# The opening of a transformer layer's kernel, written as one fixed list of steps on three engines

## The chip, the cores and the metric

The kernel runs as one program on one core of a Trainium2 chip. A core has a matrix engine (TensorE, PE in the profile), a vector engine (VectorE, DVE), a scalar engine (ScalarE, ACT), GpSimd (POOL) and queues for DMA, most of them issued here from SyncE (SP). Each engine works through its own instructions in the order in which they stand in the program, and waits on semaphores for the others.

The metric is device time in microseconds (us) of one launch. Before the change three runs took 3028.93, 3019.19 and 3015.33 us: a median of 3019.19 us.

## The reference, cut to what matters

One layer of a diffusion backbone: 2048 latent tokens and 256 context tokens of width 1024. Only its start matters here:

```python
mod_x = silu(c) @ w_mod + b_mod                    # shift, scale, gate rows
sh1, sc1, g1, sh2, sc2, g2 = split(mod_x, 6)
h_x = rmsnorm(x, norm1_g) * (1 + sc1) + sh1        # modulate
p_x = h_x @ w_in                                   # 1024 x 3840: K | V | Q | u | v | two gates
k_x = rope(rmsnorm(p_x[:, :128])); v_x = p_x[:, 128:256]
q_x = rope(rmsnorm(p_x[:, 256:768]))
...                                                # attention, gMLP, gates, output, MLP
```

## The kernel before

**The tiling.** Tokens go in blocks of 512. The input projection multiplies two blocks at a time by a 2 x 2 scheme of seven products instead of eight (Strassen's, in Winograd's form): the two token blocks are the rows of the scheme, the two halves of the 1024 inner elements are its inner index, and two neighbouring groups of columns are its columns. The first column group pair is K, V and Q, 768 columns as two of 384 (`pairs[0]`, tile width n = 384). The products are taken in the order `SUMS = (0, 1, 5, 6, 4, 2, 3)`. Product 0 and product 1 need only the first token block and raw weights. The third product taken (number 5), the fourth (6) and the later ones need differences of both blocks and differences of weights, which VectorE makes.

**Split operands.** Every fp32 factor goes to TensorE as a rounded high part (a ScalarE copy with rounding) and a low part (a VectorE subtraction of the high part), and each product of tiles is three matmuls: high by high, high by low, low by high. One product is done in two chunks of two 128-row pieces of the inner index each, and a chunk has 2 x 4 token tiles x 3 = 24 matmuls of 128x384.

**What the opening has to do before the first product.** The modulation rows are made in four quarters q = 0 to 3 (two 128-channel pieces each): 8 narrow matmuls over `w_mod` (`mod_row`, L345), a ScalarE copy of the row (L349), 4 transposes (L207 from `mod_finish`), a VectorE reduction and three small VectorE steps that leave shift S1 and scale G1 (L357 to L368). Then the 1024 channels of the normalized first block are turned, 128 channels by 512 tokens at a time: 4 transposes into one PSUM bank (`turn`, L207), then a ScalarE pass that applies G1 and S1 on the way out (L558). ScalarE and VectorE split the result (`operand`, L593 and L594), and TensorE multiplies. For the second block ScalarE first squares 8 half rows (L526), VectorE makes the inverse root (13 small steps, L172 to L188, L533) and scales 8 half rows (L543), and then the block is turned in the same way. Differences of the blocks are L604 and L605 (`h_five`), weight differences L642, their split L652 and L654.

**PSUM.** Four banks (tag `a`) hold the four token tiles of the product that runs; four (tag `b`) take everything else in turn: modulation rows, transposes, filling matmuls. Filling matmuls (`fill`, L202: ones by the identity) are put in where TensorE would otherwise stand still. Between products a partial sum is copied out of the `a` banks (L745 for product 0, L750 for products 5 and 6); after product 1 each token tile is copied out (L2255), sent to HBM (L2259, issued on ScalarE's queue) and the bank is loaded again with the sum of product 0 (L748).

**What sets the order.** `project` writes the opening as a generator, `opening()`, whose pieces are taken one by one by `pairs_run` through `hook`, between the matmuls of the first products. The instructions recorded in `self.pins` keep the order in which they are written on every engine; SP's loads keep theirs (`self.loads`). `self.fences` closes the stretch: what comes after stays behind it on TensorE and VectorE. The pinned stretch ends with the operands of product 5. After it the weight differences of product 6 and 3 and their stores (L658, from where later chunks are read back at L731) and the operands of product 6 (`h_sums`) are recorded as ordinary work.

**Loads.** SP issues in the order: head, first block x0, then for each quarter a 384 KB piece of `w_in` (L715) and 8 pieces of `w_mod` of 256 KB (L332), with the second block x1 ahead of quarter 2, and last the 16 pieces of `w_in` for the weight differences (L636). Each load waits on one of eight semaphores in turn, and so for the load eight places ahead of it.

Of the kernel before, what the change touches and what calls it, by code (L numbers as in the profile page):

```python
# [2 lines left out]

# [7 lines left out]
F32R = mybir.dt.float32r  # L11
# [59 lines left out]
LAST_ON_VECTOR = (2, 4, 7, 8, 9, 12, 13, 14, 15)  # L71

# [9 lines left out]
class Kern:  # L82
# [253 lines left out]
    def mod_row(self, w, ahead=0, between=0):  # L336
# [11 lines left out]
        row = self.t2([TB])  # L348
        nc.scalar.copy(row, ps)  # L349
        return row, pt  # L350

    def mod_finish(self, row, pt, q):
        nc = self.nc
        bcol, gcol = self.mod_cols
        self.transposes(pt, [row[:, j * P : (j + 1) * P] for j in range(2 * MQ)])
# [159 lines left out]
    def h_scale(self, xs, dve=False):  # L515
        for _ in self.h_apply(xs, self.h_rstd(xs, self.h_squares(xs)), dve):
            pass

    def h_squares(self, xs):
        nc = self.nc  # L520
        nt, parts = len(xs), len(xs[0])
        ss = self.small([parts, TT])
        for t in range(nt):
            for n, x in enumerate(xs[t]):
                junk = self.t2([D], mybir.dt.bfloat16)[:, : x.shape[-1]]
                nc.scalar.activation(junk, x, AF.Square, accum_out=ss[:, n, t : t + 1])  # L526
        return ss
# [10 lines left out]
    def h_apply(self, xs, r, dve):  # L538
        nc = self.nc
        for t in range(len(xs)):  # L540
            for x in xs[t]:
                if dve:
                    nc.vector.tensor_scalar(  # L543
                        out=x, in0=x, scalar1=r[:, t : t + 1], scalar2=None, op0=ALU.mult
                    )
                else:
                    nc.scalar.activation(x, x, AF.Copy, scale=r[:, t : t + 1])
                yield

# [4 lines left out]
    def turn(self, xs, k, out, fill=0):  # L554
        ps = self.bank([TB])
        self.fill(ps, fill)
        self.transposes(ps, [self.columns(x, k) for x in xs])
        self.nc.scalar.activation(  # L558
            out, ps, AF.Identity, scale=self.G1[:, k, 0:1], bias=self.S1[:, k, 0:1]
        )  # L560
# [47 lines left out]
    def h_sums(self, raw, h, fives):  # L608
        tt = self.nc.vector.tensor_tensor
        for k0 in range(0, HK, 2):  # L610
            for kk in (k0, k0 + 1):
                if fives:
                    self.h_five(raw, h, kk)
            yield
        for p, i, j in ((6, 0, 0), (4, 1, 0), (2, 0, 1), (3, 1, 1)):
# [10 lines left out]
    def opening_terms(self, pair, direct):  # L626
        nc = self.nc
        tt, sub = nc.vector.tensor_tensor, ALU.subtract
        n, w = pair.n, self.I["w_in"][0]
        b, t = {}, {}  # L630
        for kk in range(HK):
            for k in (kk, kk + HK):
                r = [self.h2([n]) for _ in range(2)]
                for j in range(2):
                    lo = pair.lo + j * n
                    nc.sync.dma_start(r[j], w[k * P : (k + 1) * P, lo : lo + n])  # L636
                b[k] = [r[j] for j in pair.cols]
        yield

        def term(p, kk, in0, in1):  # L640
            t[p, kk] = self.sb("hx", [n])
            tt(out=t[p, kk], in0=in0, in1=in1, op=sub)  # L642

        def first(kk):
            term(4, kk, b[kk][1], b[kk][0])
            term(5, kk, b[kk + HK][1], t[4, kk])

        def split(p, c):
            hi, lo = self.f4([2, n], F32R), self.f4([2, n], F32R)
            direct.append([(hi[:, s], lo[:, s]) for s in range(2)])  # L650
            for s in range(2):
                nc.scalar.copy(hi[:, s], t[p, 2 * c + s])  # L652
            for s in range(2):
                tt(out=lo[:, s], in0=t[p, 2 * c + s], in1=f32(hi[:, s]), op=sub)  # L654

        def store(p):
            for kk in range(HK):
                nc.sync.dma_start(self.t_d[pair.index][p][kk // 2][kk % 2], t[p, kk])  # L658

        first(0)  # L660
        yield
        first(1)
        yield
        split(5, 0)
        yield
        first(2)
        first(3)
        yield
        split(5, 1)
# [1902 lines left out]
```

## Time and profile before

| | us |
|---|---|
| runs: median, lowest, highest | 3019.19, 3015.33, 3028.93 |
| the profiled execution's own time | 3016.04 |
| its span (first to last instruction) | 3013.9 |
| TensorE busy in the span | 2938.2 (97%) |
| VectorE busy | 2084.8 (69%) |
| ScalarE busy | 1420.9 (47%) |
| GpSimd busy | 662.1 (22%) |
| DMA queue q1, share of 16 engines | 53.7% |

TensorE is busy nearly all the time, so its idle time is where the time is to be looked for. The page's row of 40 slices (75 us each) shows it for TensorE: 7 tenths in the first slice, 8 in the second, 9 (90% or more) in all others.

### The profile page before, as it was taken

Reading aid. Unit: us, or ns where it says so; the run is one execution under the profiler, and the core shown is the slowest. Engines: PE = TensorE matmul, PEld = TensorE weight load, DVE = VectorE, ACT = ScalarE, POOL = GpSimd, SP = SyncE. Lnnn points to the kernel's source line nnn. Section 1 sums busy time; section 2 is a strip of 40 time slices with the busy share of each in tenths; the row PEclk is TensorE's granted clock in tenths of the full one; section 3 lists DMA queues with packets and bytes.
Section 4 is the critical chain, followed back from the end, with each engine's and each line's share of the span. In section 5 each row is a group of like instructions: output and inputs, shape, how many; then the busy total and the mean of one; then the engine's idle time right before and its main releaser. Section 6 shows DMA issues by size and latency. Waiting matters only on the chain. (4 is left out here: it accounts for less than half of the span.)

```text
span 3013.9 us, 38296 instructions
## 1 busy us (share of the span) xinstructions
PE 2938.2 (97%) x13489; PEld 2227.6 (74%) x13489; DVE 2084.8 (69%) x2998; ACT 1420.9 (47%) x2328; POOL 662.1 (22%) x470
## 2 busy tenths in 40 slices
PE   7899999999999999999999999999999999999999
PEld 6778888876555555546888878888887888888887
DVE  4867387766888898897555587776676766654555
ACT  5645765554544545554222354444454344444432
POOL 0000000000999899895111200000000000000000
PEclk9999999999999999999999999999999999999999
DMA  7587967775010010116776658888766544447554
GB/s 268 169 298 247 321 212 217 249 245 178 24 36 27 24 37 22 30 39 195 225 219 190 184 196 306 302 306 304 260 218 223 185 154 154 154 160 270 210 209 155
DMA packets 386720, 559.06 MB, mean 185 GB/s; under 512 B 38672, under 2 KB 192448, under 8 KB 386528
## 3 DMA queue, kind: packets, MB, share of 16 engines
q1 hardware_dynamic: 374224, 535.90, 53.7%
q10 hardware_dynamic: 12304, 20.71, 1.8%
q8 instruction: 106, 1.74, 0.2%
q14 instruction: 86, 0.70, 0.1%
HBM read 379.75 MB, written 176.69 MB: 185 GB/s over the span
## 5 line engine op out<-in xcount | busy, mean ns | idle before, releaser
L2387 DVE TENSOR_REDUCE ts<-b 128x1 f32<-128x512 f32 x492 | 302.0, 683 | 62.2 <-PE b L2376 62.2
L2472 POOL TENSOR_TENSOR ac<-ac,p 128x512 f32<-128x512 f32 x214 | 317.0, 1511 | 46.4 <-ACT p L2444 46.4
L1990 DVE TENSOR_TENSOR b<-b,b 128x1024 fp32r<-128x1024 f32 x170 | 200.9, 1222 | 138.2 <-ACT b L1989 137.9
L1989 ACT CAST b<-b 128x1024 fp32r<-128x1024 f32 x170 | 170.7, 1051 | 225.8 <-PE b L1874 100.1
L2444 ACT ACTIVATE p<-b 128x512 f32<-128x512 f32 x384 | 193.5, 625 | 166.6 <-PE b L2440 158.8
L1873 PE MATMUL b<-b,b 128*128 128x512 f32 x680 | 265.3, 390 | 3.8 <-DVE b L1990 3.8
L1872 PE MATMUL b<-b,b 128*128 128x512 f32 x680 | 266.2, 391 | 2.7 <-DVE f L2011 1.4
L1874 PE MATMUL b<-b,b 128*128 128x512 f32 x680 | 264.7, 389 | 0.0
L2472 POOL TENSOR_TENSOR ac<-p,p 128x512 f32<-128x512 f32 x32 | 54.9, 1736 | 748.6 <-ACT p L2444 748.5
L2472 POOL TENSOR_TENSOR ac<-ac,t 128x512 f32<-128x512 f32 x152 | 202.7, 1361 | 0.0
L2421 PE MATMUL b<-h,h 128*128 128x512 f32 x576 | 185.9, 403 | 2.1 <-ACT m L2303 0.9
L2452 PE MATMUL b<-p,h 128*64 128x512 f32 x768 | 184.8, 604 | 0.0
L2440 PE MATMUL b<-h,h 128*128 128x512 f32 x576 | 178.1, 390 | 0.0
L1873 PE MATMUL b<-hb,b 128*128 128x512 f32 x446 | 173.8, 390 | 0.0
L1882 DVE TENSOR_TENSOR f<-f,b 128x512 f32<-128x512 f32 x160 | 109.3, 683 | 79.9 <-issue 46.3
L1872 PE MATMUL b<-hb,b 128*128 128x512 f32 x415 | 161.9, 390 | 0.9 <-DVE f L1882 0.9
L1874 PE MATMUL b<-hb,b 128*128 128x512 f32 x415 | 161.3, 389 | 0.0
L1873 PEld LDWEIGHTS b<-b,b 128*128 128x128 f32 x680 | 127.7, 188 | 32.4 <-DVE b L1990 5.8
L1872 PEld LDWEIGHTS b<-b,b 128*128 128x128 f32 x680 | 127.6, 188 | 31.1 <-ACT b L1989 3.9
L2421 PEld LDWEIGHTS b<-h,h 128*128 128x128 f32 x576 | 103.4, 188 | 61.4 <-DVE ts L2387 24.3
L1874 PEld LDWEIGHTS b<-b,b 128*128 128x128 f32 x680 | 127.6, 188 | 26.4
L166 POOL TENSOR_TENSOR bw<-bw,bw 128x512 fp32r<-128x512 f32 x58 | 76.3, 1336 | 235.6 <-ACT bw L162 235.6
(451 smaller groups left out, 7278.3 us busy)
## 6 DMA issues: line engine op xcount, KB each, us to landing
ao_d<-f SPq DMA_DIRECT2D x224, 256.0 KB
f<-in_w_ff SPq DMA_DIRECT2D x48, 1024.0 KB
b<-ao_d SPq DMA_DIRECT2D x85, 512.0 KB
b<-w2o_d SPq DMA_DIRECT2D x85, 512.0 KB
w2o_d<-f SPq DMA_DIRECT2D x112, 256.0 KB
f<-in_w_in SPq DMA_DIRECT2D x38, 512.0 KB
f<-x_d SPq DMA_DIRECT2D x64, 256.0 KB
hb<-ao_d SPq DMA_DIRECT2D x54, 256.0 KB
```

The lines of the kernel that those rows point to most:

```text
L1872: mm(ps, wh, hh, start=start and k == 0, stop=False, skip_group_check=True)
L1873: mm(ps, wh, hl, start=False, stop=False, skip_group_check=True)
L1874: mm(ps, wl, hh, start=False, stop=k == len(w) - 1, skip_group_check=True)
L1882: nc.vector.tensor_tensor(out=out, in0=in0, in1=in1, op=op)
L1989: nc.scalar.copy(h, f32(l))
L1990: nc.vector.tensor_tensor(out=l, in0=f32(l), in1=f32(h), op=ALU.subtract)
L2387: nc.vector.tensor_reduce(out=self.mx[:, t, h, c : c + 1], in_=ps[h], axis=AX.X, op=ALU.max)
L2421: self.nc.tensor.matmul(self.pts[j][h], k.KA[c][self.kv][:, ks], self.qa[h], start=True, stop=False, skip_group_check=True,)
L2440: self.nc.tensor.matmul(s, k.KB[c][self.kv][:, ks], self.qb[h], start=False, stop=True, skip_group_check=True,)
L2444: self.nc.scalar.activation(pt[h], s, AF.Exp)
L2452: nc.tensor.matmul(self.o[h * HD : (h + 1) * HD, :], k.V[c][:, i, self.kv * HD : (self.kv + 1) * HD], pt[h], start=j == 0, stop=j == NKT - 1,)
L2472: nc.gpsimd.tensor_tensor(out=self.acc[e][:, h], in0=old[:, h], in1=pt[h], op=ALU.add)
```

## The change

The generator is gone. A new method `opening(pair)` issues the same loads, defines one small function for every kind of step, and then walks a list of names, `OPENING`. All of it is pinned, and the fence stands behind it.

The names (the digits are quarter, piece or token tile):

- `fc`, `fl`: high and low part of a quarter's `w_in` piece; `rp`, `rc`, `rt`, `G`: a quarter's modulation row (matmuls, copy, transposes, reduction)
- `Ta`, `a`: transposes of the first block and the ScalarE pass behind them; `Ah`, `Al`: high and low part; `Ph`, `Pl`: matmuls of products 0 and 1 with the high part (8) and the low part (4)
- `sq`, `r`, `ap`: squares, inverse root and scaling of the second block; `Ts`, `s`: its transposes and ScalarE passes
- `d`, `t`: differences of the blocks; `Fh`, `Fl`: operands of product 5; `Eh`, `El`: operands of product 6
- `w4`, `w5`, `w6`, `w3`: weight differences; `wc`, `wl`: split of those of product 5; `vc`, `vl`: of product 6; `st`: stores of one product's differences
- `tk`: the copy out of an `a` bank after product 0 or 5; `lv`: copy out and reload after product 1; `ld`: its DMA to HBM; `Q`: the 6 matmuls of product 5 for one chunk and token tile; `z`: n filling matmuls

Operands and weight pieces of product 6 are now made in the list, as are the weight differences of product 3. `pairs_run` begins with product 6 (`begun = 6` steps). The four tiles that leave after product 1 take two buffers of tag `f4` instead of four of tag `t2`. The filling matmuls in the opening go from 46 to 37. No other instruction is added or taken away: VectorE has 3000 instructions in both programs, ScalarE 2405, SP 1740, GpSimd 472. From the end of the list on, the four streams of TensorE, VectorE, ScalarE and SP hold the same instructions in the same order in both; what is moved lies in places 42 to 252 of TensorE's, 34 to 131 of VectorE's, 15 to 104 of ScalarE's and 70 to 90 of SP's.

```diff
+OPENING = """
+fc.0 fl.0 rp.0 fc.1 fl.1 rc.0 rt.0 G.0 Ta.0.0 z.3 Ta.0.1 a.0.0 a.0.1 Ah.0.0 Ah.0.1
+Al.0.0 Ph.0.0 Al.0.1 rp.1 Ph.0.1 rc.1 rt.1 Pl.0.1 G.1 Ta.1.0 sq.2 Ta.1.1 sq.1 Pl.0.0 z.4
+a.1.0 sq.0 Ah.1.0 sq.7 Al.1.0 Ph.1.0 sq.5 sq.4 Pl.1.0 z.2 sq.6 sq.3 a.1.1 r rp.2 fc.2
+Ah.1.1 fc.3 Ph.1.1 Al.1.1 rc.2 ap.0 ap.4 rt.2 ap.2 Pl.1.1 G.2 Ta.2.0 tk.1 ap.6 Ta.2.1
+tk.0 ap.5 Ts.0.1 a.2.0 ap.1 Ts.0.3 fl.2 s.0.1 Ts.0.0 Ah.2.0 ap.7 rp.3 d.1 tk.2 s.0.0
+Al.2.0 a.2.1 ap.3 Ts.0.2 d.0 rc.3 Ts.1.0 w4.0 tk.3 rt.3 Ah.2.1 fl.3 Ph.2.0 s.1.0 G.3
+Al.2.1 Ta.3.1 Ta.3.0 w4.1 a.3.1 Pl.2.0 t.0 s.0.3 Ts.1.1 w5.1 a.3.0 Ph.2.1 d.3 Ah.3.1
+w4.2 Ah.3.0 w5.0 Ts.1.3 Fh.0 Al.3.1 Ph.3.1 s.1.3 Al.3.0 s.1.1 w5.2 Ph.3.0 w4.3 st.4 wc.0
+t.1 wc.1 wc.2 t.3 Pl.3.1 Fh.1 w5.3 s.0.2 Pl.3.0 Fl.1 wc.3 Pl.2.1 wl.0 Fh.3 wl.1 Ts.1.2
+lv.0 Fl.0 lv.1 wl.2 Q.5.0.0 Fl.3 s.1.2 d.2 Q.5.0.1 lv.2 wl.3 t.2 lv.3 Q.5.0.2 w6.0 Fh.2
+w6.2 Q.5.0.3 ld.1 Fl.2 ld.3 ld.0 w3.0 vc.0 Q.5.1.0 w3.2 Eh.0 w6.3 ld.2 w6.1 Eh.1 Q.5.1.1
+w3.3 tk.0 w3.1 vc.1 vc.3 vl.0 Q.5.1.2 tk.1 vl.1 Eh.3 El.1 Eh.2 Q.5.1.3 El.0 tk.2 El.2
+vc.2 vl.2 tk.3 El.3 vl.3
...
+    def opening(self, pair):
+        tt, sub, add = nc.vector.tensor_tensor, ALU.subtract, ALU.add
+        toks = [slice(t * P, (t + 1) * P) for t in range(TT)]
+        at = self.here()
+        wm, loaded = [], []
+        for q in range(4):
+            if q == 2:
+                x1 = self.x_load(self.x_block(1), TT, lambda n: self.sb("hx", n), 2)
+            loaded.append(self.pair_load(pair, q // 2, q % 2))
+            wm.append(self.mod_weights(q, "h" if q > 1 else "hx"))
```

```diff
...
+        def fc(q):
+            hi["w", q] = self.f4([2, n], F32R)
+            nc.scalar.copy(hi["w", q], loaded[q][0])
...
+        def rp(q):
+            v["ps", q], v["pt", q] = self.mod_row(wm[q], 0 if q else 24, 0 if q else 4)
...
+        def product(part, q, i):
+            for t, ps in enumerate(pair.ps):
+                x = hi["A", q, i] if part is high else lo["A", q, i]
+                w = hi["w", q][:, i], loaded[q][1][:, i]
+                for m in w if part is high else w[:1]:
+                    nc.tensor.matmul(
+                        ps, x[:, toks[t]], m, start=t not in begun, stop=part is low,
+                        skip_group_check=True,
+                    )
+                    begun.add(t)
+
+        def tk(t):
+            nc.scalar.copy(v["u"][t][:, 0, :n], pair.ps[t])
+
+        def lv(t):
+            if ("two", t // 2) not in v:
+                v["two", t // 2] = self.f4([2, TB])
+            v["x", t] = v["two", t // 2][:, t % 2, :n]
+            nc.scalar.copy(v["x", t], pair.ps[t])
+            nc.scalar.copy(pair.ps[t], v["u"][t][:, 0, :n])
+
+        def ld(t):
+            pair.leave_to(0, 0, t, v["x", t], nc.scalar)
...
+        def Q(p, c, t):
+            five = [operand("F", kk) for kk in (2 * c, 2 * c + 1)]
+            x = [tuple(y[:, toks[t]] for y in o) for o in five]
+            w = [(half(hi, p, kk), half(lo, p, kk)) for kk in (2 * c, 2 * c + 1)]
+            self.product(pair.ps[t], x, w, False)
+
+        def z(n):
+            self.fill(self.bank([TB]), n)
...
+        pair.ps = [self.bank([TB], tag="a")[:, :n] for _ in range(TT)]
+        v["u"] = [self.t4([2, TB]) for _ in range(TT)]
+        for step in OPENING:
+            name, *digits = step.split(".")
+            do[name](*map(int, digits))
+        self.pins.append(range(at, self.here()))
+        self.fences.append(range(at, self.here()))
+        for p in (3, 6, 5):
+            store(p)
...
+            raw[1, kk] = Joined([raw[1, j, kk] for j in range(2)])
+        h = [None] * 7
+        for j in range(2):
+            h[j] = [operand("A", *divmod(kk + j * HK, MQ)) for kk in range(HK)]
+        h[5], h[6] = operands("F"), operands("E")
+        return raw, h, v["u"], pieces(6)
...
+        for pair in pairs:
+            pair.begin(0)
+        raw, h, u, ready = self.opening(pairs[0])
+        self.work += pairs[0].ends[1]()
+
+        def context():
+            for _ in range(CONTEXT_AT - 12):
                 yield
             yield from self.context_keys()
 
-        opens = opening()
+        opens = context()
...
-                self.pairs_run(some, h, ready, along, direct if not blk and not run else None)
+                early = not blk and not run
+                self.pairs_run(some, h, ready, along, 6 if early else 0, u if early else None)
```

Three places show how the order moves. **ScalarE, the first quarter.** The rows start at the high part of the first `w_in` piece (f from f); t from b is the copy of quarter 0's modulation row, m from b the pass of a turned tile, h from m its high part. Before:

```order
L733 CAST f_89_588<-f_25_464 128x768
L349 COPY t_92_629<-b_592 128x512
L558 ACTIVATE m_640<-b_641,S_74,G_73 128x512
L593 CAST h_652<-m_640 128x512
L558 ACTIVATE m_656<-b_657,S_74,G_73 128x512
L593 CAST h_663<-m_656 128x512
L733 CAST f_106_683<-f_35_483 128x768
```

and with the change:

```order
L660 CAST f_97_596<-f_25_464 128x768
L660 CAST f_100_637<-f_35_483 128x768
L671 COPY t_101_640<-b_600 128x512
L686 ACTIVATE m_665<-b_651,S_74,G_73 128x512
L686 ACTIVATE m_667<-b_660,S_74,G_73 128x512
L698 CAST h_669<-m_665 128x512
L698 CAST h_671<-m_667 128x512
```

The high part of the second `w_in` piece (`fc.1`) moves from behind the first two tiles to ahead of the row copy, and both passes now stand ahead of both high parts.

**ScalarE, the end of product 1 and the start of product 5.** Here a is a product's bank, t_128 and the like the saved sum of product 0, p_d the HBM tensor; h from t is the high part of an operand of product 5, t from b a pass of the second block. Before:

```order
L593 CAST h_1002<-t_173_999 128x512
L558 ACTIVATE t_176_1014<-b_1015,S_74,G_73 128x512
L558 ACTIVATE t_176_1014<-b_1021,S_74,G_73 128x512
L2255 COPY t_179_1028<-a_667 128x384
L2259 DMA p_d_0_129<-t_179_1028 128x384
L748 COPY a_667<-t_128_758 128x384
L2255 COPY t_180_1033<-a_668 128x384
L2259 DMA p_d_0_129<-t_180_1033 128x384
L748 COPY a_668<-t_129_759 128x384
L2255 COPY t_181_1038<-a_669 128x384
L2259 DMA p_d_0_129<-t_181_1038 128x384
L748 COPY a_669<-t_130_760 128x384
```

and with the change:

```order
L698 CAST h_1029<-t_182_1018 128x512
L686 ACTIVATE t_167_951<-b_892,S_74,G_73 128x512
L793 CAST f_183_1021<-hx_1031 128x384
L698 CAST h_1047<-t_184_1023 128x512
L731 COPY f_191_1055<-a_588 128x384
L732 COPY a_588<-t_93_592 128x384
L731 COPY f_191_1055<-a_589 128x384
L732 COPY a_589<-t_94_593 128x384
L686 ACTIVATE t_177_995<-b_1050,S_74,G_73 128x512
L731 COPY f_195_1080<-a_590 128x384
L732 COPY a_590<-t_95_594 128x384
L731 COPY f_195_1080<-a_591 128x384
```

The DMA issues no longer stand between a tile's copy out and its reload, and three of the four high parts of product 5 stand ahead of the four tiles (the first of them above these rows), where it was two.

**VectorE, the third product's weights and operands.** L642 (L772 with the change) is a weight difference, L654 (L796) the low part of a pair's weight pieces, L604 and L605 (L764 and L768) the differences of the blocks, L594 (L702) the low part of an operand. Before:

```order
L642 TENSOR_TENSOR hx_1047<-h_573,h_572 128x384
L642 TENSOR_TENSOR hx_1049<-h_577,hx_1047 128x384
L642 TENSOR_TENSOR hx_1051<-h_581,h_580 128x384
L642 TENSOR_TENSOR hx_1053<-h_585,hx_1051 128x384
L654 TENSOR_TENSOR f_191_1081<-hx_1049,f_190_1080 128x384
L654 TENSOR_TENSOR f_191_1081<-hx_1053,f_190_1080 128x384
L604 TENSOR_TENSOR m_719<-m_719,t_176_1014 128x512
L605 TENSOR_TENSOR t_192_1086<-t_187_1055,m_719 128x512
L594 TENSOR_TENSOR h_1090<-t_192_1086,h_1089 128x512
L604 TENSOR_TENSOR m_730<-m_730,t_176_1014 128x512
L605 TENSOR_TENSOR t_195_1093<-t_187_1055,m_730 128x512
L594 TENSOR_TENSOR h_1097<-t_195_1093,h_1096 128x512
```

and with the change:

```order
L772 TENSOR_TENSOR hx_1010<-h_581,h_580 128x384
L768 TENSOR_TENSOR t_182_1018<-t_160_923,m_667 128x512
L768 TENSOR_TENSOR t_184_1023<-t_177_995,m_775 128x512
L772 TENSOR_TENSOR hx_1031<-h_585,hx_1010 128x384
L702 TENSOR_TENSOR h_1038<-t_182_1018,h_1029 128x512
L796 TENSOR_TENSOR f_188_1045<-hx_976,f_181_1016 128x384
L796 TENSOR_TENSOR f_188_1045<-hx_958,f_181_1016 128x384
L702 TENSOR_TENSOR h_1058<-t_166_949,h_983 128x512
L796 TENSOR_TENSOR f_193_1062<-hx_1000,f_183_1021 128x384
L702 TENSOR_TENSOR h_1070<-t_184_1023,h_1047 128x512
L764 TENSOR_TENSOR m_742<-m_742,t_167_951 128x512
L796 TENSOR_TENSOR f_193_1062<-hx_1031,f_183_1021 128x384
```

Before, the low parts of the second chunk's weights (L654) stand ahead of the differences for that chunk. With the change the differences and the low parts of operands and weights alternate, and the eight weight differences for products 4 and 5 stand ahead of the last of them. On SP, not shown, the first read-back of stored weight differences (product 4, L731, L893 with the change) stood behind 12 of the 16 stores and stands behind all 16.

More of the change, by code (lines that the diff above doesn't have):

```diff
@@ L347, in mod_row, with mod_finish @@
             )
[L348 to L352, printed above, removed]
+        return ps, pt
+    def mod_finish(self, pt, q):
         nc = self.nc
         bcol, gcol = self.mod_cols
-        self.transposes(pt, [row[:, j * P : (j + 1) * P] for j in range(2 * MQ)])
         part = self.small([2 * MQ, 2])
@@ L648, in split @@
[L648 to L654, printed above, removed]
+        self.loads.append(range(at, self.here()))
+        at = self.here()
+        raw, v, hi, lo, term = {}, {}, {}, {}, {}
+        begun = set()
@@ new lines, in z @@
+        def z(n):
+            self.fill(self.bank([TB]), n)
+        do = {
+            f.__name__: f
+            for f in (fc, fl, rp, rc, rt, G, Ta, a, tk, lv, ld, sq, r, ap, Ts, s, d, t, w3, w4, w5, w6, Q, z)
+        }
+        do["st"] = store
+        for name, f in (("A", A), ("F", F), ("E", E), ("P", product)):
+            do[name + "h"], do[name + "l"] = partial(f, high), partial(f, low)
+        for name, p in (("w", 5), ("v", 6)):
+            do[name + "c"], do[name + "l"] = partial(cast, p), partial(rest, p)
```

327 lines of the change are left out of this document (129 added, 198 removed).

## The prediction

> **What bounds the kernel now.** I read the waits of TensorE first, then busy time by stage, then the timelines of the opening. The two waits (total, times, longest) that tell most:
>
> ```profile
> PE a L1872 <- ACT a L748: 6.4, 1, 6.4
> PE a L1873 <- DVE f L734: 2.0, 1, 2.0
> ```
>
> ```profile
> core 0: us, PE busy (x) PEld busy (x) DVE busy (x) ACT busy (x) POOL busy (x), PEclk, DMA share, GB/s
> 42.00:89.00 47.00, 34.72 (x206) 30.43 (x205) 30.44 (x63) 26.81 (x48) 0.00 (x0) 0.93 0.49 160
> 62.00:82.00 20.00, 10.87 (x50) 9.99 (x49) 11.60 (x21) 11.03 (x22) 0.00 (x0) 0.83 0.23 79
> 82.00:100.00 18.00, 15.21 (x81) 13.42 (x80) 18.00 (x32) 13.93 (x29) 0.00 (x0) 1.00 0.63 193
> ```
>
> Over the whole span TensorE has little to give. In the opening it has: between 62 and 82 us it works 10.87 of 20, and so do VectorE (11.60) and ScalarE (11.03). No engine is full there; the three wait for each other in turn. From 82 to 100 VectorE is full (18.00 of 18.00) and is the bound. Between 42 and 89 it stands idle for 47 - 30.44 = 16.56 us.
>
> ```profile
> 68.80 0.69 PE L1872 MATMUL a<-f,h 128*128 128x384 f32 x1 [6.43 <-ACT a L748]
> 77.49 0.44 PE L1872 MATMUL a<-f,h 128*128 128x384 f32 x1 [2.36 <-ACT h L593]
> 99.83 0.44 PE L1873 MATMUL a<-f,h 128*128 128x384 f32 x1 [2.04 <-DVE f L734]
> 74.43 1.03 DVE L654 TENSOR_TENSOR f<-hx,f 128x384 fp32r<-128x384 f32 x2 [5.46 <-ACT f L652]
> 88.91 1.89 DVE L620 TENSOR_TENSOR t<-t,t 128x512 f32<-128x512 f32 x3
> 98.83 0.95 DVE L734 TENSOR_TENSOR f<-f,f 128x768 fp32r<-128x768 f32 x1
> ```
>
> At 68.80 the third product begins, 6.43 us late, because the reload after product 1 (L748) stands behind other passes on ScalarE; at 74.43 VectorE has stood 5.46 us for a copy (L652) that stands behind the same reloads; 77.49 repeats it in small. At 88.91 VectorE begins the first step (L620) that both programs hold in the same place: there I compare. From it VectorE runs without a gap to the low part at 98.83, for which TensorE waits at 99.83.
>
> **The change part by part.** *Up to the copy of quarter 2's modulation row.*
>
> ```profile
> 12.77 0.83 ACT L733 CAST f<-f 128x768 fp32r<-128x768 f32 x1 [0.26 <-DMA f<-in_w_in]
> 19.36 0.59 ACT L349 COPY t<-b 128x512 f32<-128x512 f32 x1 [5.75 <-PE b L345]
> 40.96 0.59 ACT L349 COPY t<-b 128x512 f32<-128x512 f32 x1
> L332 SPq DMA_DIRECT2D hx<-in_w_mod x16: 327/328/465, 8.1 to 19.2; - x16
> L332 SPq DMA_DIRECT2D h<-in_w_mod x16: 327/328/328, 27.3 to 38.8; - x16
> ```
>
> A load is issued when the one eight places ahead of it has landed. So the `w_in` piece of quarter 1 is there at 19.2, and that of quarter 3 at 38.8 (the last `w_mod` issues of quarters 1 and 3 stand eight places behind them). ScalarE's cast `fc.1` now stands ahead of the row copy `rc.0`: it waits to 19.2, takes 0.83, and the copy starts at 20.0 instead of 19.36. The price, 0.6 us, is hidden by the loads. Row copy, transposes and reduction end at 22.0, two passes and a high part at 24.2, and the 11.6 us of TensorE's steps between that and quarter 2's row (by the durations below) end near 36; but the last `w_mod` piece of quarter 2 lands near 38, one issue of 0.7 ahead of 38.8. Then `fc.3` waits to 38.8 and the copy `rc.2` starts at 38.8 + 0.7 = 39.5, against 40.96. This stretch is bound by loads, which do not move: gain 1.4. The 9 filling matmuls that go stood ahead of these loads, and so give nothing.
>
> *From there to the common step.* Issue to issue, one step takes:
>
> ```profile
> 42.22 2.06 DVE L543 TENSOR_SCALAR hx<-hx,ts 128x512 f32<-128x512 f32 x5
> 44.20 0.18 DVE L357 TENSOR_REDUCE ts<-b 128x8 f32<-128x32 f32 x1
> 44.69 0.16 DVE L368 SCALAR_TENSOR_TENSOR G<-G,ts 128x4 f32<-128x4 f32 x1
> 80.78 1.96 DVE L642 TENSOR_TENSOR hx<-h,h 128x384 f32<-128x384 f32 x4
> 82.66 2.05 DVE L654 TENSOR_TENSOR f<-hx,f 128x384 fp32r<-128x384 f32 x4
> 84.63 0.68 DVE L594 TENSOR_TENSOR h<-m,h 128x512 fp32r<-128x512 f32 x1
> 85.23 0.55 DVE L642 TENSOR_TENSOR hx<-h,hx 128x384 f32<-128x384 f32 x1
> 38.75 1.58 ACT L745 COPY t<-a 128x384 f32<-128x384 f32 x4
> 57.36 1.44 ACT L558 ACTIVATE t<-b,S,G 128x512 f32<-128x512 f32 x2
> 67.37 0.47 ACT L2255 COPY t<-a 128x384 f32<-128x384 f32 x1
> 67.87 0.36 ACTq L2259 DMA_DIRECT2D p_d<-t  x1
> 68.27 0.48 ACT L748 COPY a<-t 128x384 f32<-128x384 f32 x1 [0.43 <-ACT t L2255]
> 81.93 0.93 ACT L652 CAST f<-hx 128x384 fp32r<-128x384 f32 x2
> 84.70 1.69 ACT L593 CAST h<-m 128x512 fp32r<-128x512 f32 x3
> 48.71 1.92 PE L345 MATMUL b<-h,t 128*32 128x512 f32 x16
> 50.98 1.64 PE L778 MATMUL a<-f,h 128*128 128x384 f32 x8
> 54.05 1.03 PE L207 MATMUL b<-ident,t 128*128 128x128 f32 x8
> 60.55 0.95 PE L785 MATMUL a<-f,h 128*128 128x384 f32 x4
> ```
>
> VectorE: `rc.2` at 39.5 ends at 40.1, its transposes at 40.6, and the reduction `G.2` (0.65, rows 44.20 and 44.69) at 41.3. Behind it in the list stand 5 scalings of 0.41, 2 low parts of weights of 0.95, 8 differences of 0.61 (1.89 for three in row 88.91), 12 low parts of operands of 0.60 (84.63 to 85.23), 16 weight differences of 0.47, 8 low parts of 0.50 and one reduction of 0.65: 2.05 + 1.9 + 4.9 + 7.2 + 7.5 + 4.0 + 0.65 = 28.2. Without a wait it would be through at 69.5.
>
> ScalarE from 39.5: 8 bank copies of 0.39, 12 passes of 0.72, 12 high parts of 0.53, 8 casts of 0.42, 8 copies of the reload of 0.48, 4 DMA issues of 0.36, 2 row copies of 0.59: 3.1 + 8.6 + 6.4 + 3.4 + 3.8 + 1.4 + 1.2 = 27.9, to 67.4. TensorE from 41.4: 12 turned tiles of 0.43, a modulation row of 1.9, its transposes 0.5, four `Ph` of 1.5, four `Pl` of 0.8 and 48 matmuls of 0.18 (row 50.98: 8 in 1.64 with the tail of the last) for product 5: 5.2 + 1.9 + 0.5 + 6.0 + 3.2 + 8.6 = 25.4, to 66.8. The three are within 3 us of each other, so a wait of any one tells.
>
> Now the waits, by the longest path through the list, each step starting when its engine is free and its inputs are there. Product 1's first half ends on TensorE at 40.6 + 0.8 = 41.4. ScalarE then does two bank copies, `a.2.0`, `s.0.1`, `Ah.2.0`, a bank copy, `s.0.0` and `a.2.1` (4.7 with 0.1 for a dependent step) and reaches the row copy `rc.3` at 46.1; the row's matmuls ran from 43.8, when a bank was free, to 45.7 (48.71 before). The copy ends at 46.7, the transposes at 47.2; `G.3` follows a low part and ends at 48.1. `Ta.3.1` stands behind `Ph.2.0` (47.2 to 48.7), so `a.3.1` runs from 49.25 to 50.0. From there ScalarE has no gap: 5 passes, 5 high parts and 4 casts, 3.6 + 2.65 + 1.7 = 7.9, bring it to the reloads at 57.9, which TensorE has just made possible (product 1 ends there too). Eight copies and one pass, 3.8 + 0.7, end at 62.4, and `Fh.2` at 63.0. VectorE, 0.6 idle before it, goes on: `Fl.2` and six weight differences to 66.4, two low parts each of weights and operands to 68.6, the last four, with 0.25 of waiting for ScalarE, to 71.1. Product 5 runs from 59.0 to 67.9. So **71.1 instead of 88.91: 17.8 us**; VectorE's waits are 1.6 over its 28.2.
>
> This path is too smooth. A step on another engine starts about 0.05 after its releaser (98.83 + 0.95 = 99.78, to 99.83), and the list changes engine some 30 times along it, twice that if each step beside it counts: 0 to 3 us. I take 2.0, leaving 15.8.
>
> ```profile
> 83.33 0.37 SPq L731 DMA_DIRECT2D f<-t_d  x1
> 86.61 0.84 ACT L733 CAST f<-f 128x768 fp32r<-128x768 f32 x1 [0.23 <-DMA f<-t_d]
> ```
>
> *After the common step.* VectorE's list is the same; it needs 9.92 us (88.91 to 98.83) to the low part that TensorE awaits: 71.1 + 9.9 + 0.95 = 82.0. TensorE needs product 6 (8.6) from 67.9, one chunk of product 4 (4.3) and 4 matmuls (0.7): 81.5. So VectorE still leads and the whole gain arrives. The cover to watch is the read-back of product 4's weights: it landed 3.28 us after its issue (83.33 to 86.61). It now stands on SP behind all 16 stores, the last of which wait for `w3.1` at 66.4; issued near 68 it lands at 71.3, and ScalarE reaches it at 72.4. The cover is 1.1 us; beyond it each us late costs one. The buffer that it needs (two more `f4` tiles are now in the rotation) is free when product 5's first chunk ends at 63.6. What follows hangs on these chains and on loads issued by them, so it shifts as one.
>
> **Sum.** 3016.04 (the profiled execution, span 3013.9 and 2.1 around it) - 17.8 + 2.0 = 3000.2. The median of the three runs is 3.15 above the profiled time; I add a quarter of this: **3001.0**.
>
> **Rivals.** *A, in-order waits.* The list is pinned on all engines, so a late input stops all three: `fc.1` and `fc.3` show it. For: in the pinned stretch before, VectorE idled 16.56 of 47. Against: the sums leave little room for idling, and loads are early after 45 us. If half the idle time returns, 8.3 us of 17.8 are lost: 3006.5 to 3008.
>
> *B, given back at product 4.* If the read-back comes as late as its whole 3.28 us beyond the cover on both chunks (6.6) on top of the forecast: 3007.6. For: four more stores ahead of it. Against: the DMA share from 62 to 82 is 0.23.
>
> *C, the clock stays full.*
>
> ```profile
> 100.30 0.52 PE L1872 MATMUL a<-f,h 128*128 128x384 f32 x1
> 104.45 0.33 PE L1872 MATMUL a<-f,h 128*128 128x384 f32 x1
> ```
>
> After the gap of 2.04 us at 99.83, matmuls take 0.52 instead of 0.33 for some 3.5 us, which loses half of that, 1.75; after 2.36 us at 77.49 the first takes 0.44. If the shorter wait of the walk there (82.0 - 81.5) spares the drop and TensorE leads behind it: 2999.2. The Trainium skill ("TensorE: Matmul & The Clock Gate", section "Why this matters for your kernels") asks for idle gaps under about 3 us to keep the full clock. By that rule no wait of the walk would cost a drop and C would hold; the trace shows a drop behind a single gap of 2.04 us, so I don't count it in the sum.
>
> *D, slower: half clock through the opening.* Fewer filling matmuls, and early waits (1.5 us at 23, some 2 spread over 36 to 38) could let the clock fall and stay low to product 5. TensorE's work from 23 to 68 is about 40 us at full clock; at half it adds 40: 3041. To end slower than before, nine drops of 1.75 must follow each other; with eight the gain is eaten. Against: the same stretch had 16 us of idle time and one long drop.
>
> That the list moves nothing is excluded: the streams differ as written.
>
> **How the numbers follow.** A measurement of this kernel tells a change of about 0.5% (15 us) from none. Forecast (2996 to 3007): 0.60, of which 0.45 lies more than 15 us below the median (under 3004), 0.15 not. A: 0.20, with 0.03 faster. B: 0.12, same. C: 0.05, faster. D: 0.03, slower. Faster 0.53, same 0.44, slower 0.03. The range 2994 to 3011 goes from C without the loss for hand-offs and some to A with a median 3 us above the profile.
>
> **What would show it.** Right: the common step (L627 with the change) near 73; product 5 from 59 to 62; the gap of 6.43 gone; a wait of ScalarE for a load at 19.2 and 38.8; PEclk 1.00 from 42 to 82. Wrong: VectorE idle for over 5 us between 42 and the common step; a wait for the read-back ahead of product 4; matmuls at 0.52 ahead of product 5.

## Result and the profile after

The changed kernel takes 2993.6 us (median of five undisturbed runs, 2989.2 to 2997.2; a sixth, of 15529.7 us, is left out), against 3019.8 for the kernel before, measured beside it: ratio 0.9906 (of the two medians 0.9913), 95% interval 0.9884 to 0.9928. A second comparison, with 17 runs of the kernel before (median 3015.3), gave 0.9928 (0.9912 to 0.9943), that is 21.7 us (17.2 to 26.5). The profiled execution took 2994.62 us (span 2992.8), 21.4 less than that of before. The prediction said 3001.0, from 2994 to 3011: the direction and the mechanism hold, the size was put too small by 7.4 us, and the time lies just below the range.

The stretches of the opening, from the table by stage of the changed kernel (columns as in the prediction):

```profile
core 0: us, PE busy (x) PEld busy (x) DVE busy (x) ACT busy (x) POOL busy (x), PEclk, DMA share, GB/s
...
24.00:38.00 14.00, 13.81 (x91) 10.08 (x92) 4.28 (x18) 9.36 (x24) 0.00 (x0) 1.00 1.06 385
...
42.00:62.00 20.00, 19.22 (x131) 16.82 (x130) 19.55 (x40) 18.75 (x36) 0.00 (x0) 1.00 0.77 256
62.00:82.00 20.00, 19.85 (x114) 19.29 (x113) 19.64 (x34) 16.31 (x32) 0.00 (x0) 1.00 0.65 220
82.00:100.00 18.00, 15.37 (x100) 14.74 (x98) 15.05 (x48) 6.24 (x10) 0.00 (x0) 1.00 0.76 232
```

From 62 to 82 us TensorE works 19.85 of 20 (10.87 before), VectorE 19.64 (11.60), ScalarE 16.31 (11.03), and the granted clock is 1.00 (0.83). From 42 to 62 all three are busy for 94% or more. From 24 to 38 the transfers are full (share 1.06): that stretch is still bound by loads.

The steps of the walk, from the timelines of the changed kernel ("the common step" is the first VectorE step that stands in the same place in both programs, L620 before and L627 after):

```profile
19.25 0.83 ACT L660 CAST f<-f 128x768 fp32r<-128x768 f32 x1 [5.64 <-DMA f<-in_w_in]
...
38.88 0.84 ACT L660 CAST f<-f 128x768 fp32r<-128x768 f32 x1 [1.06 <-DMA f<-in_w_in]
...
39.63 0.58 ACT L671 COPY t<-b 128x512 f32<-128x512 f32 x1
...
40.98 0.19 DVE L371 TENSOR_REDUCE ts<-b 128x8 f32<-128x32 f32 x1 [0.69 <-PE b L224]
...
50.57 0.69 DVE L764 TENSOR_TENSOR m<-m,t 128x512 f32<-128x512 f32 x1 [0.21 <-ACT t L686]
...
58.39 0.44 PE L1913 MATMUL a<-f,h 128*128 128x384 f32 x1 [0.62 <-ACT a L732]
...
62.36 0.69 DVE L702 TENSOR_TENSOR h<-t,h 128x512 fp32r<-128x512 f32 x1 [0.53 <-ACT h L698]
...
70.07 1.89 DVE L627 TENSOR_TENSOR t<-t,t 128x512 f32<-128x512 f32 x3
...
71.56 0.84 ACT L895 CAST f<-f 128x768 fp32r<-128x768 f32 x1 [0.16 <-DMA f<-t_d]
...
80.98 0.44 PE L1914 MATMUL a<-f,h 128*128 128x384 f32 x1 [0.15 <-DVE f L896]
```

The casts wait for loads at 19.25 and 38.88, as foretold. From 40.98 to the common step VectorE waits twice, 0.21 and 0.53 us; between the same two steps of the kernel before (44.20 and 88.91) its waits add up to 16.0. Product 5 begins at 58.39 after a wait of 0.62 (6.43 before). The common step stands at 70.07 instead of 88.91: 18.84 us, where the forecast had 15.8. ScalarE waits 0.16 us for the read-back of product 4's weights, and TensorE's wait of 2.04 at the end of this stretch is one of 0.15. Behind it the two programs are the same on every engine. There the shift does not stay put. The same steps of VectorE in both: 160.03 and 140.41 (19.62), 327.48 and 314.13 (13.35), 1414.61 and 1400.68 (13.93); at the end it is 3013.9 - 2992.8 = 21.1.

### The profile page after: what moved, and what is told of

Its sections match the earlier page's. It is cut to its first block, busy times and chain, and to the rows that moved or that the text cites. A ratio compares the mean times of both kernels' runs of the same rounds, so it can differ in the third digit from the quotient of the medians.

```text
span 2992.8 us, 38248 instructions
## 1 busy us (share of the span) xinstructions
PE 2932.9 (98%) x13471; PEld 2223.6 (74%) x13471; DVE 2082.9 (70%) x2998; ACT 1419.8 (47%) x2328; POOL 661.4 (22%) x470
## 4 chain that ended last, share of the span: by engine, by line
PE 83%; DVE 6%; DMA 6%; ACT 2%; issue 1%; SPq 0%; ACTq 0%; DVEq 0%
PE b L1913 14%; PE b L1914 14%; PE b L1915 14%; PE b L2496 8%; PE b L2465 4%; PE b L2484 4%; PE b L212 4%; PE b L213 4%; PE b L214 4%; PE b L2420 3%; PE a L1913 2%; PE a L1915 2%; PE a L1914 2%; PE b L224 1%; DVE ts L2431 1%
## 5 line engine op out<-in xcount | busy, mean ns | idle before, releaser
L2465 PEld LDWEIGHTS b<-h,h 128*128 128x128 f32 x576 | 103.5, 188 | 60.1 <-DVE ts L2431 24.3
L1926 ACT ACTIVATE f<-f 128x512 f32<-128x512 f32 x96 | 60.5, 630 | 148.7 <-DVE f L1923 148.7
```

Source lines behind the costliest of these rows:

```text
L2465: self.nc.tensor.matmul(self.pts[j][h], k.KA[c][self.kv][:, ks], self.qa[h], start=True, stop=False, skip_group_check=True,)
```

## Experiments

The changed kernel's common step and span are 70.07 and 2992.8; the difference of the two is called the rest (2922.7; before: 2925.0). All medians are to be read beside 2993.6 for the changed kernel, which it had again in the first group.

**The two kernels again.** Nothing is changed.

> The kernel before, unchanged. Two theories of the 2.3 us that the changed program gained behind the common step (its rest, from there to the end of the span, is 3013.9 - 88.91 = 2924.99 before and 2992.8 - 70.07 = 2922.73 after). Theory J (jitter): what follows the common step has the same length in both programs, and the gains and losses there are loads that come late in one execution and not in another. The common step lies at 88.9 within 0.3 again, the rest anywhere from 2924 to 2938 (the runs shown go from 3015.3 to 3028.9 us), and places between 165 and 215 us or behind 1400 us move by some us against the first profile of the same kernel. Rival P (phase): the rest is longer in the program before because its loads fall otherwise; it is then again 2925 within 1, and every place agrees with the first profile within 0.5 us.

> The changed kernel, unchanged. J: common step at 70.1 within 0.3, rest from 2917 to 2927 or more (the runs shown go from 2989.2 to 2997.2 us), with the loss of 5.3 us between 140 and 210 us not repeated in the same size. P: rest 2922.7 within 1, the loss of 5.3 us there again.

| | common step | span | rest | median us |
|---|---|---|---|---|
| before again | 88.96 | 3011.4 | 2922.4 | 3013.5 |
| changed again | 70.30 | 2994.1 | 2923.8 | 2993.6 |

The opening repeats to 0.2 us. The rest does not: the kernel before moved by 2.5 us, the changed one by 1.1 the other way, which turns the 2.3 us gained behind the common step into a loss of 1.4. J holds in kind, though the rest of the kernel before came out below the 2924 to 2938 that it allowed; P falls. Between VectorE's steps at 140.41 and 203.62 the changed kernel took 63.2 us in its first execution and 60.9 in its second, the kernel before 58.6 and 59.5. One such place is a wait of TensorE near 187 us for an operand made of `w_in` pieces, in the first and in the second execution of the changed kernel:

```profile
187.47 1.09 PE L224 MATMUL b<-ident,m 128*128 128x128 f32 x4 [4.05 <-DVE m L1004]
```

```profile
186.25 0.91 PE L224 MATMUL b<-ident,m 128*128 128x128 f32 x4 [2.28 <-DVE m L1004]
```

In the kernel before it is 1.62 in the first execution and 0.28 in the second. Loads and stores are dense there, as the table by stage of the changed kernel shows: share 0.88 over 45 us, with TensorE at 39.71 of 45.20.

```profile
145.40:190.60 45.20, 39.71 (x171) 31.88 (x170) 22.23 (x42) 15.50 (x27) 0.00 (x0) 0.95 0.88 305
```

**3.5 to 4.7 us more on one engine.** Three kernels, each with extra work (the lines of the list are shown in part): `x.8` makes `w4.0`'s difference eight times more (VectorE, at 47 us), or `wc.0`'s cast (ScalarE, at 55), `z.14` is 14 fills (TensorE, at 48).

```diff
-rc.3 Ts.1.0 w4.0 tk.3
+rc.3 Ts.1.0 w4.0 x.8 tk.3
...
-st.4 wc.0
+st.4 wc.0 x.8
...
-fl.3 Ph.2.0
+fl.3 z.14 Ph.2.0
```

> The changed kernel with 8 more differences of 128x384 on VectorE at the step w4.0 (0.47 each, 3.8 us; they write the same result again). Theory F (all three engines are full from 41 to 70 us, so each us put on any of them arrives): common step at 70.1 + 3.8 - 0.2 = 73.7, the chunk of product 4 on TensorE (80.98) at 84.6, span some 3.6 us longer, as far as jitter lets it be seen. Rival S (slack: an added us is taken up by waits behind it): common step below 72.

> The changed kernel with 8 more casts of 128x384 on ScalarE at the step wc.0 (0.42 each, 3.4 us; they write the same result again). F: the first reload copy from 57.3 to 60.7, product 5 from 58.4 to 61.8, common step at 70.1 + 3.4 = 73.5. Rival V (VectorE alone is the bound; ScalarE and TensorE have room, as their busy times of 18.8 and 19.2 of 20 against 19.6 might leave): common step moves by under 1.5.

> The changed kernel with 14 more filling matmuls pairs on TensorE ahead of Ph.2.0, at 47 us (0.25 each, 3.5 us). F: all of TensorE behind it is later, product 1 ends 3.5 later, product 5 begins at 61.4 to 61.9 instead of 58.4, the common step lies at 73. V: it moves by under 1.5. The prediction's sums gave TensorE 25.4 us of work in 25.4 + 2.8, so up to 1 us may be taken up.

The timelines of the three, in this order:

```profile
46.82 4.71 DVE L823 TENSOR_TENSOR hx<-h,h 128x384 f32<-128x384 f32 x8
...
75.25 1.89 DVE L627 TENSOR_TENSOR t<-t,t 128x512 f32<-128x512 f32 x3
```

```profile
54.74 4.33 ACT L823 CAST f<-hx 128x384 fp32r<-128x384 f32 x8
...
62.95 0.69 PE L1917 MATMUL a<-f,h 128*128 128x384 f32 x1 [4.95 <-ACT a L732]
...
75.29 1.89 DVE L627 TENSOR_TENSOR t<-t,t 128x512 f32<-128x512 f32 x3
```

```profile
47.72 3.39 PE L219 MATMUL b<-ident,ones 128*128 128x128 f32 x28 [0.59 <-DVE ts L371]
...
73.96 1.90 DVE L627 TENSOR_TENSOR t<-t,t 128x512 f32<-128x512 f32 x3
```

All three arrive in full at the common step: +5.2 for 4.7 us on VectorE, +5.2 for 4.3 on ScalarE, +3.9 for 3.4 on TensorE. F holds; the rivals S and V fall. The extra work was itself priced too low (0.58 us for a difference made again into the same tile, not 0.47; 0.53 for a cast). The 0.5 to 0.9 us by which more arrives than was put in was not followed up; in the first two TensorE also worked at half clock, behind waits of 3.50 and 4.95 us. The medians are 2994.7, 2996.1 and 2994.9, only 1.1 to 2.5 above the changed kernel's: with four runs each and a rest that moves by some us they do not tell 4 or 5 us for certain.

**The same work put into an idle time of the kernel before.**

```diff
         first(2)
         first(3)
+        for _ in range(8):
+            tt(out=t[4, 2], in0=b[2][1], in1=b[2][0], op=sub)
         yield
```

> The kernel before with 8 more differences of 128x384 on VectorE (3.8 us, the same result written again) behind those that end at 68.9 us, where VectorE then stands idle for 5.46 us until 74.43. Theory (before, the engines wait for each other in turn, so work put into an idle time is free; the change fills these times): common step at 88.9 within 0.3. Rival: the order of before is as tight as the changed one, and the 3.8 us arrive: 92.7. In the changed kernel the same 3.8 us moved the common step by 5.2.

```profile
68.89 4.70 DVE L669 TENSOR_TENSOR hx<-h,h 128x384 f32<-128x384 f32 x8
74.43 1.03 DVE L654 TENSOR_TENSOR f<-hx,f 128x384 fp32r<-128x384 f32 x2 [0.84 <-ACT f L652]
...
88.91 1.89 DVE L620 TENSOR_TENSOR t<-t,t 128x512 f32<-128x512 f32 x3
```

This is VectorE's timeline of that kernel. The wait of 5.46 us shrinks to 0.84 and nothing moves behind it: the common step is at 88.91 to the hundredth (median 3012.8). The same eight differences cost 5.2 us after the change and nothing before. That is what the change did: it filled these times.

**One part undone: each high and low part right behind the difference that it is made of.**

```diff
-a.3.1 Pl.2.0 t.0 s.0.3
-w4.2 Ah.3.0 w5.0 Ts.1.3 Fh.0 Al.3.1
-Ts.1.2 lv.0 Fl.0 lv.1
+a.3.1 Pl.2.0 t.0 Fh.0 Fl.0 s.0.3
...
```

(One of the four operands is shown.)

> The changed kernel with one thing undone: the high part Fh and the low part Fl of each of product 5's four operands stand right behind the difference t that they are made of, on VectorE and ScalarE, as in the order before, instead of several steps away. Theory (the gain is the distance between a step and its user): VectorE waits 0.7 us for each Fh and ScalarE up to 1 us for each t; common step 2 to 3 us later, 72.1 to 73.1, and 1.5 more if a wait of TensorE over 2 us halves the clock. Rival: other steps cover it; within 0.5 of 70.1.

VectorE's and TensorE's timelines (rows of four pairs; the first matmul of product 5 and the next two):

```profile
50.69 0.69 DVE L701 TENSOR_TENSOR h<-t,h 128x512 fp32r<-128x512 f32 x1 [0.69 <-ACT h L697]
...
56.82 0.69 DVE L701 TENSOR_TENSOR h<-t,h 128x512 fp32r<-128x512 f32 x1 [0.69 <-ACT h L697]
...
58.80 0.69 DVE L701 TENSOR_TENSOR h<-t,h 128x512 fp32r<-128x512 f32 x1 [0.68 <-ACT h L697]
...
64.50 0.69 DVE L701 TENSOR_TENSOR h<-t,h 128x512 fp32r<-128x512 f32 x1 [0.74 <-ACT h L697]
...
73.61 1.89 DVE L626 TENSOR_TENSOR t<-t,t 128x512 f32<-128x512 f32 x3
```

```profile
61.45 0.56 PE L1912 MATMUL a<-f,h 128*128 128x384 f32 x1 [3.32 <-ACT a L731]
61.81 0.53 PE L1913 MATMUL a<-f,h 128*128 128x384 f32 x1
62.13 0.53 PE L1914 MATMUL a<-f,h 128*128 128x384 f32 x1
```

Four waits of 0.7 us, 2.8 in all, and the common step is 3.5 us later, at 73.61: the theory holds with its addition for the clock, since TensorE waited 3.32 us and worked at 0.62 from 62 to 66 us. A hand-off costs where the user comes next in order, and there VectorE waits 0.7 us, the other engine's whole pass (0.62) and some 0.1. The median, 2991.7, does not show the 3.5 us.

**The two row copies ahead of the casts that wait for loads.**

```diff
-rp.0 fc.1 fl.1 rc.0
+rp.0 rc.0 fc.1 fl.1
-Ah.1.1 fc.3 Ph.1.1 Al.1.1 rc.2
+Ah.1.1 Ph.1.1 Al.1.1 rc.2 fc.3
```

> The changed kernel with the casts fc.1 and fc.3, which wait for loads at 19.2 and 38.8, put behind the row copies rc.0 and rc.2. Theory (the prediction's): the first costs nothing, since loads bound what follows; the second costs 0.7: the row copy rc.2 at 38.95 instead of 39.63, common step at 69.4. Rival: nothing, since the cast then delays the first bank copies by as much; common step at 70.1 within 0.1.

The common step came later instead, at 71.49, for a reason in neither theory. A row of TensorE's timeline of this kernel, and a stretch of its table by stage (PEclk, the third number from the end, is the granted clock):

```profile
25.08 2.93 PE L718 MATMUL a<-f,h 128*128 128x384 f32 x8 [2.13 <-ACT h L698]
```

```profile
26.00:29.00 3.00, 3.00 (x15) 1.82 (x17) 0.36 (x1) 0.00 (x0) 0.00 (x0) 0.59 1.06 386
```

The gap of 2.13 us comes from the edit. `fl.1`, the low part of the second `w_in` piece, still stands ahead of the reduction of quarter 0, and now waits for a cast that runs behind the row copy, as VectorE's timeline of this kernel shows:

```profile
21.46 0.96 DVE L664 TENSOR_TENSOR f<-f,f 128x768 fp32r<-128x768 f32 x1 [2.21 <-ACT f L660]
```

The reduction follows at 22.33 instead of 21.32, while the row copy is no earlier (20.11, and 19.99 in the changed kernel). Eight matmuls that take 1.69 us in the changed kernel take 2.93 here: behind the gap the granted clock fell to 0.59. The row of quarter 2 began at 37.99 instead of 35.62 and ended 1.0 us later (39.91 and 38.92), its copy began at 40.09 instead of 39.63. So the prediction's "price 0.6, hidden by the loads" is neither shown nor refuted; what shows is that of a delay of 2.4 us the loads hide 1.4 there, not all. The median is 2992.4.

**The stores of the leaving halves right behind their reloads.**

```diff
-lv.0 Fl.0 lv.1 wl.2
+lv.0 ld.0 Fl.0 lv.1 ld.1 wl.2
...
-Q.5.0.3 ld.1 Fl.2 ld.3 ld.0 w3.0
+Q.5.0.3 Fl.2 w3.0
...
```

> The changed kernel with each store of a leaving half (ld) right behind its reload (lv), as the order before had it, so that ScalarE issues four DMAs (0.36 each) ahead of Fh.2 instead of one. F: three more issues ahead of Fh.2 are 1.1 us, VectorE waits for it, common step at 71.1, and product 5's third and fourth bank later by 0.7. Rival: an issue costs the engine nothing while the stores drain; common step at 70.1 within 0.2.

ScalarE's timeline of this kernel:

```profile
57.79 0.48 ACT L732 COPY a<-t 128x384 f32<-128x384 f32 x1
57.79 0.34 ACTq L2303 DMA_DIRECT2D p_d<-f  x1
58.20 0.47 ACT L731 COPY f<-a 128x384 f32<-128x384 f32 x1
...
61.68 0.62 ACT L698 CAST h<-t 128x512 fp32r<-128x512 f32 x1
```

The issue runs beside the reload, and the next copy follows 0.41 us after it, as without an issue. `Fh.2` starts at 61.68 (61.72 in the changed kernel), the common step is at 70.03: the rival holds. This is not quite the order before, which issued between the copy out and the reload. What that order paid was this place: there the issue waited for the copy (67.37 to 67.87 in the prediction's rows) and the reload came 0.9 us after the copy instead of 0.5. Nor is an issue always free: in the changed kernel two follow each other behind `Fh.2`, and ScalarE stands still for 0.56 us (no wait is named but the issue):

```profile
61.78 1.06 ACTq L2303 DMA_DIRECT2D p_d<-f  x2
62.89 0.52 ACT L793 CAST f<-hx 128x384 fp32r<-128x384 f32 x1 [0.56 <-issue]
```

**No fills at all.** `rp` without its 28, and every `z` gone.

> The changed kernel without any of the 37 filling matmul pairs of the opening (nothing of the result is left out). Rival D of the prediction (the clock drops and stays low where TensorE has gaps): matmuls at twice their time from 15 us on, common step later by 5 us or more. The other side: the stretch to 41 us is bound by loads and the one behind has no gaps, so the common step stays at 70.1 within 1, even with some half-clock matmuls ahead of 38 us.

The common step is at 70.58, 0.5 later; from 24 to 38 us the granted clock is 0.88 and TensorE works 13.02 of 14, and from 42 to 70 the clock is 1.00. D falls: the clock drops for a short time only, and in a stretch in which the transfers are full (share 1.06). Median 2992.1.

**The common step as late as before.** 40 differences in the place of the 8 above.

> The changed kernel with 40 more differences of 128x384 on VectorE at the step w4.0 (18.8 us), so that its common step comes as late as in the kernel before: 70.1 + 18.8 and 1.5 for half-clock matmuls behind TensorE's wait (the 3.8 us of e3 arrived as 5.2) = 90.4. Theory I: what follows the common step takes 2921 within 4, as in the changed kernels so far (2918.5 to 2925.4 by their spans), whenever it starts: about 3013 us. Rival A: the rest depends on when it starts, and the kernel before is longer there (its times less its common step are some 5 us above those of the changed kernels) because it starts 18.85 us later: about 3017 us.

The 40 took 23.7 us, not 18.8, and the common step came at 94.31. Rest 2914.1, median 3016.7; less the common step the median is 2922.3, against 3015.3 - 88.9 = 2926.4 for the kernel before and 2993.6 - 70.2 = 2923.4 for the changed one. A falls: a late start does not make the rest longer. I is supported, though the rest of this profile is shorter than the 2917 to 2925 that it allowed.

**More fills at the next gap.** TensorE waits 2.5 us at 100.5 us in the changed kernel.

```diff
-self.fill(ps.rearrange("p j c -> p (j c)"), 18)
+self.fill(ps.rearrange("p j c -> p (j c)"), 26)
```

> The changed kernel with 26 instead of 18 filling matmul pairs ahead of the first transposes of the context keys (8 more, 0.25 us each: 2.0 us). TensorE waits 2.5 to 3.3 us there at 100.5 us, and works at half clock for some 3 us behind it. Theory (the wait is filled, the clock stays up): the gap falls to 0.5 to 1.3, no matmuls at half speed behind it, and the later places (VectorE at 140) come 1.5 us earlier. Rival: the products behind the fills come 2 us later and with them what waits for their end, so nothing is won or up to 1 us lost.

The table by stage of the changed kernel, and then of this one:

```profile
100.00:104.00 4.00, 1.49 (x4) 0.61 (x4) 2.04 (x4) 4.00 (x7) 0.00 (x0) 0.60 0.37 115
104.00:108.00 4.00, 3.52 (x13) 3.53 (x14) 4.00 (x8) 0.87 (x4) 0.00 (x0) 0.54 0.21 75
```

```profile
100.00:104.00 4.00, 2.11 (x12) 1.58 (x11) 2.52 (x3) 4.00 (x7) 0.00 (x0) 1.00 0.46 135
104.00:108.00 4.00, 4.00 (x30) 4.00 (x30) 3.77 (x8) 1.82 (x5) 0.00 (x0) 1.00 0.34 122
```

The clock stays at 1.00, and VectorE's step at 140.41 comes at 138.25, 2.2 us earlier. Not all of this is the fills'. ScalarE's wait for a read-back, ahead of the gap, ended 0.74 us earlier in this execution (first row: the changed kernel, second: this one; 96.25 when the changed kernel ran again):

```profile
96.11 0.83 ACT L895 CAST f<-f 128x768 fp32r<-128x768 f32 x1 [6.20 <-DMA f<-t_d]
```

```profile
95.37 0.83 ACT L895 CAST f<-f 128x768 fp32r<-128x768 f32 x1 [5.50 <-DMA f<-t_d]
```

The other 1.4 us were won behind the gap, where the half speed is gone. The gap itself was expected at 0.5 to 1.3 us and only fell from 2.53 to 2.01. Elsewhere a gap of 2.04 us did cost a slow stretch, so the length alone does not say that the fills kept the clock up; where the gap lay may have done it (last section). The gain is in one trace; the median of 2989.8 (ratio to the kernel before 0.9918, 0.9902 to 0.9935) does not set this version apart from the changed kernel.

## Why the prediction was right in kind and too small in size

*What bounds the kernel before* was read rightly. The engines waited for each other in turn: 4.6 us of VectorE's work put into its idle time were free there, and 3.4 to 4.7 us put on any engine of the changed order arrived in full.

*Up to quarter 2's row:* the casts' waits at 19.2 and 38.8 and the row copy at 39.5 came within 0.15 us. That loads bound this stretch is borne out by the kernel without fills.

*From there to the common step* is the step that failed, by its size: 18.84 us instead of 15.8. **The term mis-sized is the 2.0 us for hand-offs; the trace leaves nothing for it.** From quarter 2's reduction on, the forecast had 28.2 us of VectorE's work, 1.6 of waits and these 2.0; the trace has 27.8 of work and 0.74 of waits, and the stretch began 0.3 later (41.56 where the walk had 41.3). An allowance of 0.05 for each of 30 to 60 changes of engine charges every one of them, but only one whose user is next in its engine's order can be seen. In the list a step mostly stands several steps ahead of its user; put side by side, four such pairs cost 3.5 us. The walk without the allowance was still 1.0 too slow (71.1, then 70.07).

*After the common step*, "it shifts as one" was wrong in detail. TensorE stood still 0.15 us instead of 2.04 and no half-clock matmuls followed: on TensorE the shift grew from 18.9 at this step to 20.4 some 5 us later. This is rival C's mechanism, which I had left out of the sum, and it won 1.55 of the 1.75 that C named. But the loads did not come earlier by as much: ScalarE's cast of a `w_in` piece, which had waited to 103.50, now waited to 85.83 (17.67), and about half was given back, so that at 140 us the shift was 0.8 larger. Then some 6 us were given back up to 314 us and 8 came again, most of them behind 1400 us. The executions repeated do not bear out that these are the change's: the rests of all fourteen profiles lie between 2914.1 and 2925.4 us, and the three of the kernel before, one of them with work added ahead of the common step, lie among the others at 2917.4, 2922.4 and 2925.0.

*The sum:* 2994.62 profiled against 3000.2 forecast is 5.6, of which 3.0 came by the common step, 0.8 by 140 us, 1.5 behind it, and 0.3 lie around the span. The rest of the miss is the median: I put it 0.8 above the profile, and it came out 1.0 below. The kernel before had its first three runs high: 3015.3 to 3015.6 were its medians in the three later groups.

*The rivals:* A (half of the idle time returns) did not happen; from 42 us to the common step none of the three engines waits longer than 1.02 us. B was near: the cover of the read-back was gone, ScalarE waited 0.16 us for it, and nothing behind it was later for that (VectorE runs without a wait from the common step to 85 us). D fell; its count was off too, since nine drops of 1.75 are 15.75 us, not more than the forecast gain of 15.8, so that it would have taken ten to end slower. What stays open is whether the kernel before is some 3 us longer behind the common step by its median; the interval of the second comparison, 17.2 to 26.5 us, holds 18.8 alone as well as 18.8 and 3 more.

## What to carry to other kernels

Price a hand-off between engines only where the user is the next step of its engine; taken from issue to issue, durations hold the rest, and an allowance for every crossing counts what nobody waits for. Whether an order is tight can be asked directly: put 4 us of harmless work on each engine in turn and see at a common step whether they arrive. Read such a change at the first step that both programs share; the time of the whole kernel moves by more than the effect from one execution to the next.

## What the hardware did unexpectedly

The granted clock does not follow the length of one gap. TensorE worked at half speed behind gaps of 6.43, 4.95, 3.32, 2.13, 2.04 and, in the second execution of the kernel before, 1.77 us. It did not in the kernel before behind 2.36 us at 77.49 and 2.18 us at 46.42, but in the same execution it did behind another gap of 2.36:

```profile
119.84 0.33 PE L1049 MATMUL b<-ident,m 128*128 128x128 f32 x1 [2.36 <-ACT m L547]
```

Behind this one the granted clock is 0.50 from 121 to 125 us; behind that at 77.49 it is 1.00. TensorE's timeline of the kernel before where one slow stretch ends, and of the same kernel run again behind the gap of 1.77 us:

```profile
72.49 0.52 PE L1874 MATMUL a<-f,h 128*128 128x384 f32 x1
72.81 0.41 PE L1872 MATMUL a<-f,h 128*128 128x384 f32 x1
73.05 0.34 PE L1873 MATMUL a<-f,h 128*128 128x384 f32 x1
```

```profile
99.89 0.44 PE L1873 MATMUL a<-f,h 128*128 128x384 f32 x1 [1.77 <-DVE f L734]
...
100.53 0.34 PE L1873 MATMUL a<-f,h 128*128 128x384 f32 x1
100.70 0.49 PE L1874 MATMUL a<-f,h 128*128 128x384 f32 x1
...
103.86 0.47 PE L1874 MATMUL a<-f,h 128*128 128x384 f32 x1
104.17 0.33 PE L1873 MATMUL a<-f,h 128*128 128x384 f32 x1
```

In the second, work has resumed for 0.8 us when the speed falls, and it is back 3.3 us later. In the first execution slow stretches end at 72.9 and 103.5 and one begins at 100.25, that is on a grid of 3.4 us (9 and 8 steps apart). Set against this grid, the gaps of this execution that cost a slow stretch filled over half of one step (2.04 of 3.4 us at 99.83, 2.36 at 119.84), and those of 2.36 at 77.49 and 2.18 lie across an edge, with under 1.4 us on either side. The kernel with 26 fills fits: a slow stretch of its own runs from 184.4 to 187.8, and 25 steps of 3.4 us ahead of it an edge would fall near 99 us (an estimate), within its gap from 97.73 to 99.74. That is a reading of few cases, not a test. The Trainium skill ("TensorE: Matmul & The Clock Gate", section "What's actually happening") describes windows of 3.4 us that run freely, with a drop after one idle window. The length agrees with these rows; that a whole window must be idle does not.

A DMA issue of 0.34 us on ScalarE cost nothing behind an unrelated pass that was still running; of two in a row, 1.06 us together, 0.56 was seen. A 128x384 difference made again into the same tile took 0.58 us on VectorE, where four into different tiles take 1.96 together.
